# adaLN's middle weight rows in a two-layer diffusion backbone: six moved to the first branch, eighteen behind the second branch's second unit

## The chip, the cores and the metric

One core of a Trainium2 chip runs the whole program. The metric is the time of one execution on the device in microseconds; less is better. Three executions of the kernel before gave 2494.15 us at the median (2492.76 to 2498.52). The profile is of one further execution.

## The reference, cut to what matters

Two post-norm layers work on 640 tokens of width 1024 (128 context tokens, 512 latent ones). Everything is float32, and a product of two matrices is done as three products of rounded parts (high by high, high by low, low by high).

```python
sh1, sc1, g1, sh2, sc2, g2 = split(silu(cond) @ w_ada + b_ada, 6)      # adaLN, 6144 columns
h = x * (1 + sc1) + sh1
r_out, s_out, n_out = retention(h), s5(h), attention(h)               # three mixers of one projection
m = (ga * (r_out @ wb[0]) + gb * (s_out @ wb[1]) + gc * (n_out @ wb[2])) @ w_o
x = layer_norm(alpha * x + g1 * m)
x = layer_norm(alpha * x + g2 * conv_ffn(x * (1 + sc2) + sh2))
```

The condition has one vector for the context tokens (`c_ctx`) and one for the latent ones (`c`). The state-space mixer (`s5`) has a scan over 80 blocks of 8 tokens, then outputs, a gelu, and a gated unit: `y * sigmoid(y @ w_glu)`. Its result goes through the second branch product.

## The kernel before, in words

**The stream of units.** `layer` writes out a list of units. A unit names the weight tiles that it needs (128 by 1024 float32, 512 KB each) and emits its instructions. Projections (`a_unit`, `gate_unit`), the gated unit (`glu_unit`, L1262 to L1288) and branch products (`branch_unit`, L1298 to L1332) take one tile per unit; 48 matmuls of 128x320 make a unit of about 7 us on TensorE. Around the change the order is: eight gates of the first branch, its four branch units, four gates of the second branch (with `ssm_out`, the gelu of the state-space mixer, put ahead of the third), two gated units, then the four units of the second branch with the other four gates among them, then the query and key projections of the attention.

**The weight ring.** `load_to` (L202) issues the loads on the SyncE queue in the order of the list into a ring of four `raw` buffers (`NRAW`). `split_to` (L210) makes a high part on ScalarE (L176) and a low part on VectorE (L177), into three pairs of buffers (`NHL`). A tile of the kind `raw` is not split: it keeps its raw buffer until the instructions that use it are done. The next tile in the list takes whichever buffer comes free first.

**adaLN as rows.** The first 16 blocks of 128 columns of layer 0 are done by matmuls at the start. All others are done by VectorE in `ada_rows` (L297 to L314). A row unit loads one tile of `w_adaT` (two blocks of 128 columns by 512 inputs) and takes four products with sums against the two silu rows `crow` (L308, 128x512 each). Each block needs two such units, one for either half of the inputs; the second also adds to the first and the bias (L311, L312). `cond_rows(i)` (L278 to L289) makes the two rows `crow` for half `i` of the inputs: a load on the POOL queue (L285), a tanh on ScalarE (L286) and two instructions on VectorE (L287, L288) each.

**Where rows go.** `build` mixes the row units into the list by `spread`, which puts `extra` evenly behind the units of a stretch. The middle rows of a layer (blocks 16 to 39) are 26 entries: 12 units of the first half, `cond_rows(1)`, 12 units of the second half, and the release of `crow`. They begin at `s.rows_at` (L1581). Their results are needed at the third branch (`make_gate`) and at the output projection (`scales`), much later.

**The scan.** In both layers the scan of the state-space mixer is a chain of 64 steps of four VectorE instructions (L1194 to L1197). Behind it come `ssm_outputs` (copies at L1224, matmuls at L1238 and L1240, `ym` at L1241, stores at L1245) and `ssm_out` (loads at L1254, gelu at L1256, the split into `gyhi` and `gylo`), and then the gated unit (matmuls at L1273).

**The order on an engine.** The context is made with `schedule_with_timeline_sim=True`: the build gives each engine's queue its order by a timeline of its own, in which an instruction may go ahead of earlier ones of the list that aren't ready. On the chip the queue is then followed as it stands.

Of the kernel before, what the change touches and what calls it, by code (L numbers as in the profile page):

```python
# [80 lines left out]
class Kernel:  # L81
# [1389 lines left out]
    def layer(s, l):  # L1471
        nc, A, O = s.nc, s.A, s.O
        units = []
# [92 lines left out]
        for h in range(4):  # L1566
            add(s.rg_unit(l, h, need=[rets[h]]))
        for c in range(8):
            if c == 6:
                add(s.action(lambda: s.cond_rows(0)))  # L1570
            add(s.gate_unit(l, 0, c))
        for i in range(4):
            add(s.branch_unit(l, 0, i))

# [3 lines left out]
            add(s.gate_unit(l, 1, c))  # L1578
        for i in range(2):
            add(s.glu_unit(l, i))  # L1580
        s.rows_at = len(units) + 1  # L1581
        for i in range(4):
            for c in (2 * i, 2 * i + 1) if i > 1 else ():
                add(s.gate_unit(l, 1, c))
            add(s.branch_unit(l, 1, i))
        c = 0
# [134 lines left out]
    def build(s):  # L1721
        s.adac, s.bcol, s.gate, s.ret, s.ssm, s.ready = {}, {}, {}, {}, {}, set()
        s.rq, s.rk, s.rv, s.rout = {}, {}, {}, {}
        s.nq, s.nk, s.nvd, s.nout = {}, {}, {}, {}
        s.gy, s.sout, s.gts, s.hid, s.chunk = {}, {}, {}, {}, {}
        s.preps = [[None, g, r, 0] for g, r in ((s.first_ssm(), RATE_S), (s.ssm_prep(1), RATE_P))]
        s.ada_begin(0)
        s.setup()
        units = [s.hold(s.win(0, 2)[:2])]

        def first(n):
            s.ada_unit(n)
            s.first_h(n)

        for n in range(4):
            if n < 3:
                units.append(s.action(lambda n=n: s.ada_load(n + 1), start=[] if n else [s.preps[0]]))
            units.append(s.action(lambda n=n: first(n), cost=1))
        def rest():
            s.free(s.cond)  # L1740
            s.cap = len(s.slots)

        units.append(s.action(rest))
        def rows(l, a, b, first):

            r = lambda i, last: [s.ada_rows(l, m, i, last) for m in range(a // 2, b // 2)]
            return r(first, False) + [s.action(lambda: s.cond_rows(1 - first))] + r(1 - first, True)

        s.crow = []
        w = len(TURNS)  # L1750
        done = s.action(lambda: [s.free(s.crow), s.crow.clear()])
        for l in range(s.layers):
            u = [s.action(lambda l=l: s.begin(l))] + s.layer(l)
            find = lambda: [i for i, x in enumerate(u) if x["emit"].__qualname__.endswith("res_unit.<locals>.emit")]
            at = find()
            if l + 1 < s.layers:
                extra = [s.action(lambda l=l: s.ada_begin(l + 1))] + rows(l + 1, 0, 16, 0)
                u = s.spread(u, extra, at[w] + 1, at[-w])
            u = s.spread(u, [s.action(lambda: s.cond_rows(1))] + rows(l, 40, 48, 1), at[w - 1] + ADA[0], at[w - 1] + ADA[2])
            u = s.spread(u, rows(l, 16, 40, 0) + [done], s.rows_at, at[0] - 3 - ADA[1])  # L1760
            u.insert(find()[-w], done)
            units += u
        s.run(units)
# [11 lines left out]
BETWEEN = (0, 0, 0, 8)  # L1775

ADA = (14, 14, 16)

RATE_R, RATE_N, RATE_S, RATE_T, RATE_P = 2.5, 2.75, 1.25, 0.7, 0.5

# [98 lines left out]
```

## Time and profile before

| what | value |
|---|---|
| median of three runs | 2494.15 us (2492.76 to 2498.52) |
| the profiled execution | 2493.69 us |
| its span from first to last instruction | 2491.9 us |
| instructions | 44951 |
| mean granted TensorE clock | 0.983 of full speed |

The span is what the trace shows; the profiled execution's time has 1.8 us around it. In rows of the trace, PE is TensorE's matmuls, PEld its weight loads, DVE VectorE, ACT ScalarE, POOL GpSimd, SP SyncE, and a small q marks an engine's own queue. A number after x counts instructions. What stands in brackets behind `<-` is the work that ended the idle time before. Times count from the span's start.

### The profile page before, as it was taken

To read this page: it belongs to the slowest core of one execution; us is meant where nothing else is said; L and a number is where in the kernel's file an instruction comes from. 1 tells how busy PE (TensorE), PEld (TensorE's weight loads), DVE (VectorE), ACT (ScalarE), POOL (GpSimd) and SP (SyncE) were. 2 spreads that over 40 slices of the span, in tenths; PEclk is the share of its full clock that TensorE was granted. 3 is DMA by queue.
4 is the path that set the end of the run, shared out by engine and by line. 5 is a ranking of instruction groups with operands and counts; after the bars stand their busy time and mean duration, and the time that the engine had idled before them with its cause. 6 is when DMAs were issued, how large, how long until landed. Compare 5 with 4: busy or idle time off the path is not lost.

```text
span 2491.9 us, 44951 instructions
## 1 busy us (share of the span) xinstructions
PE 2391.0 (96%) x17788; PEld 2324.2 (93%) x17788; DVE 1793.1 (72%) x4241; ACT 978.4 (39%) x1713; POOL 414.1 (17%) x676
## 2 busy tenths in 40 slices
PE   6999998999999999999999999999999999999996
PEld 3998998899898999999999999999989999999996
DVE  7986765886667988899684577379667888555647
ACT  2445434245634323222345644422655333232231
POOL 5423222203200002110011120411131000000001
PEclk8999999999999999999999999999999999999998
DMA  8744445643233436444354332555333343212222
GB/s 284 249 152 132 138 130 170 189 143 104 74 97 103 140 100 222 128 159 138 122 171 130 98 111 91 160 171 190 103 92 100 107 138 97 85 57 93 90 64 81
DMA packets 108099, 324.18 MB, mean 130 GB/s; under 512 B 24848, under 2 KB 25680, under 8 KB 107888
## 3 DMA queue, kind: packets, MB, share of 16 engines
q1 hardware_dynamic: 62784, 211.32, 25.9%
q0 software_dynamic: 44672, 109.86, 14.6%
q8 instruction: 140, 2.29, 0.4%
q14 instruction: 71, 0.58, 0.1%
q10 hardware_dynamic: 432, 0.13, 0.0%
HBM read 287.09 MB, written 38.21 MB: 131 GB/s over the span
## 4 chain that ended last, share of the span: by engine, by line
PE 65%; issue 20%; DVE 9%; DMA 4%; ACT 2%; POOL 1%; POOLq 0%; DVEq 0%; ACTq 0%
PE pa L148 35%; PE pa L1311 6%; PE b L1351 2%; PE b L1352 2%; PE b L1353 2%; DMA raw<-in_w_adaT 2%; DVE lo L177 2%; PE pn L859 2%; PE pa L515 1%; PE pa L517 1%; PE pa L516 1%; PE b L757 1%; DVE junk L308 1%; PE b L846 1%; PE b L1173 1%
## 5 line engine op out<-in xcount | busy, mean ns | idle before, releaser
L148 PE MATMUL pa<-hth,hi 128*128 128x320 f32 (+2 forms) x2896 | 683.1, 314 | 21.9 <-DVE cv L1395 8.5
L148 PE MATMUL pa<-htl,hi 128*128 128x320 f32 (+2 forms) x2896 | 681.8, 313 | 3.0 <-DVE htl L396 2.1
L148 PE MATMUL pa<-hth,lo 128*128 128x320 f32 (+2 forms) x2896 | 680.6, 313 | 0.0
L176 ACT ACTIVATE hi<-raw 128x1024 fp32r<-128x1024 f32 (+1 forms) x316 | 322.2, 1022 | 850.9 <-PE pa L148 351.4
L177 DVE TENSOR_TENSOR lo<-raw,hi 128x1024 fp32r<-128x1024 f32 (+1 forms) x316 | 372.4, 1180 | 262.1 <-ACT hi L176 250.9
L148 PEld LDWEIGHTS pa<-hth,hi 128*128 128x128 f32 x2896 | 490.9, 190 | 32.5 <-issue 10.4
L148 PEld LDWEIGHTS pa<-htl,hi 128*128 128x128 f32 x2896 | 493.0, 190 | 9.9 <-DVE htl L396 3.7
L148 PEld LDWEIGHTS pa<-hth,lo 128*128 128x128 f32 x2896 | 493.6, 190 | 1.7 <-issue 1.2
L308 DVE SCALAR_TENSOR_TENSOR junk<-raw,crow 128x512 bf16<-128x512 f32 x320 | 223.3, 698 | 47.6 <-DMA raw<-in_w_adaT 44.0
L1352 PE MATMUL b<-lo,hdh 128*128 128x256 f32 x784 | 218.2, 281 | 0.0
L1353 PE MATMUL b<-hi,hdl 128*128 128x256 f32 x784 | 217.7, 281 | 0.0
L1351 PE MATMUL b<-hi,hdh 128*128 128x256 f32 x784 | 215.0, 282 | 2.2 <-ACT hi L176 2.2
L1395 DVE SCALAR_TENSOR_TENSOR cv<-pa,conv,cv 128x641 f32<-128x641 f32 (+3 forms) x180 | 153.6, 854 | 4.5 <-ACT cv L1391 2.5
L1351 PEld LDWEIGHTS b<-hi,hdh 128*128 128x128 f32 x784 | 145.8, 188 | 3.7 <-ACT hi L176 3.2
L1352 PEld LDWEIGHTS b<-lo,hdh 128*128 128x128 f32 x784 | 147.7, 189 | 0.0
L1353 PEld LDWEIGHTS b<-hi,hdl 128*128 128x128 f32 x784 | 147.4, 189 | 0.0
L1355 DVE TENSOR_TENSOR rm<-b,g 128x256 f32<-128x256 f32 x168 | 69.3, 421 | 74.4 <-PE b L1353 74.0
L515 PE MATMUL pa<-hi,hth 128*128 128x256 f32 x320 | 91.5, 287 | 2.3 <-ACT qk L1482 2.3
L516 PE MATMUL pa<-lo,hth 128*128 128x256 f32 x320 | 90.0, 282 | 0.0
L517 PE MATMUL pa<-hi,htl 128*128 128x256 f32 x320 | 89.3, 282 | 0.0
L1391 ACT ACTIVATE cv<-pa,conv 128x641 f32<-128x641 f32 (+2 forms) x90 | 76.3, 848 | 17.7 <-PE pa L148 14.5
L176 ACT ACTIVATE hdh<-cv 128x641 fp32r<-128x641 f32 x44 | 32.6, 741 | 125.4 <-DVE cv L1403 125.4
(440 smaller groups left out, 4360.9 us busy)
## 6 DMA issues: line engine op xcount, KB each, us to landing
raw<-in_w_in_a SPq DMA_DIRECT2D x96, 512.0 KB, 3.7
raw<-in_w_up SPq DMA_DIRECT2D x88, 512.0 KB, 3.6
raw<-in_w_adaT SPq DMA_DIRECT2D x80, 512.0 KB, 4.2
raw<-in_w_down SPq DMA_DIRECT2D x36, 512.0 KB, 3.5
raw<-in_w_branch SPq DMA_DIRECT2D x24, 512.0 KB, 3.8
raw<-in_w_o SPq DMA_DIRECT2D x24, 512.0 KB, 3.5
wada<-in_w_ada SPq DMA_DIRECT2D x32, 256.0 KB, 6.1
raw<-in_w_in_b SPq DMA_DIRECT2D x16, 512.0 KB, 4.6
```

The source lines that it names most:

```text
L148: s.nc.tensor.matmul(ps[h][:, :n], w[a][:, k], x[b][:, k, c0:c0 + n], start=(k == 0 and part == 0), stop=(k == nk - 1 and part == 2))
L176: s.nc.scalar.activation(hi, src, AF.Copy)
L177: return (eng or s.nc.vector).tensor_tensor(lo, src, hi.bitcast(FT), op=OP.subtract)
L308: nc.vector.scalar_tensor_tensor(junk, w[:, n], 1.0, s.crow[j], op0=OP.mult, op1=OP.mult, accum_out=acc[:, n, j:j + 1])
L515: mm(ps, h[0], x[0], start=(k == 0), stop=False)
L516: mm(ps, h[0], x[1], start=False, stop=False)
L517: mm(ps, h[1], x[0], start=False, stop=(k == 7))
L1311: nc.tensor.matmul(ps[:, h, :n], w[a][:, k, 128 * c:128 * c + 128], out[k][x][:, c0:c0 + n], start=(k == 0 and part == 0), stop=(k == 3 an ...
L1351: mm(ps, a[0], x[0], start=(k == 0), stop=False)
L1352: mm(ps, a[0], x[1], start=False, stop=False)
L1353: mm(ps, a[1], x[0], start=False, stop=(k == nk - 1))
L1395: nc.vector.scalar_tensor_tensor(x[:, o0:o1], z[:, z0:z0 + o1 - o0], cw(tap), x[:, o0:o1], op0=OP.mult, op1=OP.add)
```

## The change

Three things are edited. `cond_rows(0)`, the silu of the first half of the conditions, is put ahead of the fifth gate of the first branch rather than the seventh. `s.rows_at` becomes a list of two places: the last gate of the first branch, and the first gate behind the second branch's second unit. Of the 26 middle entries the first six row units go to the first place, one behind each of six units (the last gate, the four units of the first branch, the first gate of the second branch); the other twenty (eighteen row units, `cond_rows(1)` and the release) are spread over the twelve units from the second place on, to the same end as before. The rows themselves, their count and their order are unchanged.

```diff
         for c in range(8):
-            if c == 6:
+            if c == 4:
                 add(s.action(lambda: s.cond_rows(0)))
             add(s.gate_unit(l, 0, c))
+        s.rows_at = [len(units)]
         for i in range(4):
             add(s.branch_unit(l, 0, i))
...
         for i in range(2):
             add(s.glu_unit(l, i))
-        s.rows_at = len(units) + 1
         for i in range(4):
+            if i == 2:
+                s.rows_at.append(len(units) + 1)
             for c in (2 * i, 2 * i + 1) if i > 1 else ():
                 add(s.gate_unit(l, 1, c))
             add(s.branch_unit(l, 1, i))
...
-            u = s.spread(u, rows(l, 16, 40, 0) + [done], s.rows_at, at[0] - 3 - ADA[1])
+            middle = rows(l, 16, 40, 0) + [done]
+            u = s.spread(u, middle[EARLY:], s.rows_at[1], at[0] - 3 - ADA[1])
+            u = s.spread(u, middle[:EARLY], s.rows_at[0], s.rows_at[0] + EARLY)
...
 ADA = (14, 14, 16)
+
+EARLY = 6
```

## Rows read from the trace of the kernel before

**Rows 1.** The page, busy time of each engine

```profile
PE 2391.0 (96%) x17788; PEld 2324.2 (93%) x17788; DVE 1793.1 (72%) x4241; ACT 978.4 (39%) x1713; POOL 414.1 (17%) x676
```

**Rows 2.** Stretches: length, busy us of PE, PEld, DVE, ACT, POOL; PEclk, DMA, GB/s

```profile
350.00:400.00 50.00, 50.00 (x376) 50.00 (x375) 18.81 (x41) 30.57 (x34) 23.92 (x41) 1.00 0.53 169
...
415.00:470.00 55.00, 42.58 (x234) 40.27 (x233) 40.64 (x83) 16.38 (x20) 10.79 (x17) 0.84 0.55 160
...
1650.00:1680.00 30.00, 27.56 (x180) 26.23 (x180) 27.13 (x55) 7.74 (x11) 8.97 (x13) 1.00 0.77 208
```

**Rows 3.** Waits of TensorE, 360 to 560 us: in total, times, longest

```profile
PE pa L1311 <- DVE solo L1283: 4.2, 2, 3.4
PE pa L1273 <- DVE gylo L177: 4.0, 2, 2.9
PE pa L1273 <- ACT gyhi L176: 2.5, 2, 1.5
PE pa L1311 <- ACT sohi L1282: 1.1, 1, 1.1
PE pa L1311 <- DVE gt L1315: 0.6, 1, 0.6
```

**Rows 4.** Timeline of TensorE, 439 to 448 us: start, length, what

```profile
439.12 0.46 PE L1311 MATMUL pa<-sohi,hi 128*128 128x320 f32 x2
...
444.19 0.74 PE L1311 MATMUL pa<-sohi,lo 128*128 128x320 f32 x2
444.72 0.73 PE L1311 MATMUL pa<-sohi,hi 128*128 128x320 f32 x2
...
447.48 0.45 PE L1311 MATMUL pa<-sohi,hi 128*128 128x320 f32 x2
447.77 0.46 PE L1311 MATMUL pa<-solo,hi 128*128 128x320 f32 x2
```

**Rows 5.** VectorE's timeline: two adaLN rows' first products

```profile
392.99 0.69 DVE L308 SCALAR_TENSOR_TENSOR junk<-raw,crow 128x512 bf16<-128x512 f32 x1 [1.07 <-DMA raw<-in_w_adaT]
...
450.44 0.69 DVE L308 SCALAR_TENSOR_TENSOR junk<-raw,crow 128x512 bf16<-128x512 f32 x1 [4.80 <-DMA raw<-in_w_adaT]
```

**Rows 6.** The page, group of line 308

```profile
L308 DVE SCALAR_TENSOR_TENSOR junk<-raw,crow 128x512 bf16<-128x512 f32 x320 | 223.3, 698 | 47.6 <-DMA raw<-in_w_adaT 44.0
```

**Rows 7.** Timelines of VectorE and SyncE, 295 to 297 us

```profile
295.42 1.23 DVE L177 TENSOR_TENSOR lo<-raw,hi 128x1024 fp32r<-128x1024 f32 x1 [0.34 <-ACT hi L176]
...
296.67 0.33 SPq L206 DMA_DIRECT2D raw<-in_w_branch  x1
```

**Rows 8.** VectorE's timeline in the second layer's scan

```profile
1497.35 0.22 DVE L1197 TENSOR_TENSOR H<-H,rc 128x64 f32<-128x64 f32 x1
1497.61 0.23 DVE L1194 TENSOR_TENSOR rc<-H,ssm_ar 128x64 f32<-128x64 f32 x1
...
1498.47 0.22 DVE L1197 TENSOR_TENSOR H<-H,rc 128x64 f32<-128x64 f32 x1
1498.61 0.69 DVE L288 TENSOR_TENSOR crow<-crow,crt 128x512 f32<-128x512 f32 x1
1499.21 0.22 DVE L1194 TENSOR_TENSOR rc<-H,ssm_ar 128x64 f32<-128x64 f32 x1
```

**Rows 9.** Timelines: scan's end and last gylo in each layer; first gated matmul

```profile
354.87 0.23 DVE L1197 TENSOR_TENSOR H<-H,rc 128x64 f32<-128x64 f32 x1
...
427.85 0.82 DVE L177 TENSOR_TENSOR gylo<-gy,gyhi 128x640 fp32r<-128x640 f32 x1
...
1545.63 0.23 DVE L1197 TENSOR_TENSOR H<-H,rc 128x64 f32<-128x64 f32 x1
...
1616.10 0.82 DVE L177 TENSOR_TENSOR gylo<-gy,gyhi 128x640 fp32r<-128x640 f32 x1
...
1639.97 0.46 PE L1273 MATMUL pa<-gyhi,hi 128*128 128x320 f32 x2
```

**Rows 10.** The page, DMA issues: size each, us to landing

```profile
raw<-in_w_adaT SPq DMA_DIRECT2D x80, 512.0 KB, 4.2
```

## The prediction

> **What bounds the kernel now.** I read the page's busy times first. TensorE is busy 96% of the span [rows 1], so an edit that moves VectorE work can only win back TensorE's idle time, or add to it. Then I cut the span into stretches to see where that idle time lies. Around the change, TensorE is full from 350 to 400 us and again after 470, but from 415 to 470 it is busy 42.58 of 55 us at a granted clock of 0.84; the same place in the second layer, 1650 to 1680, loses 2.44 us at full clock [rows 2]. So the first layer's gated unit and the second branch's first units hold 12.4 us of idle time, and some slow clock. The table of waits names who is late: `gylo` and `gyhi`, the gelu's split (6.5 us), then `solo`, `sohi` and `gt`, the gated unit's output and the branch's evacuation (5.9 us) [rows 3].
>
> Third, the timeline shows what a wait costs beyond itself. Behind one, pairs of matmuls start 0.53 us apart (444.19, 444.72) where they later start 0.29 apart (447.48, 447.77) [rows 4]: the lower of the two clocks, 1.2 GHz, then the higher, 2.4. I count 6 slow pairs after 443.5 and 11 after 454.6, 17 x 0.24 = 4.1 us.
>
> Fourth, VectorE's timeline. adaLN rows stand in the list behind the second branch's first unit, whose matmuls begin at 439.12 [rows 4]; the first row runs at 392.99 [rows 5], 46 us earlier. **A unit's place in the list is thus not its place in a queue**: the build lets rows go ahead as soon as the ring has a buffer. And it seems to count on a quicker load than the chip's. VectorE sat idle 1.07 us before that row and 4.80 before the one at 450.44, with the gated unit's last `solo` queued behind it [rows 5]; over all 80 rows such waits make 44.0 us [rows 6].
>
> **The change, part by part.** *Silu sooner.* Two loads on the POOL queue, two tanh and four VectorE instructions go ahead by two gates. Ends: 0, and 4 x 0.48 = 1.9 us if they newly enter the scan (price below). I take 0: in the second layer such an instruction already stands within the scan [rows 8]. The price of a late `crow` would be rows stuck in the ring with weights queued behind them on SP.
>
> *Six rows at the first branch.* Where do they land? A freed raw buffer goes to the next tile in the list: a split ends at 295.42 + 1.23 = 296.65, and SP issues the next load, a branch weight, at 296.67 [rows 7]. In the new list the first early row stands just ahead of that weight, so it takes this load, and with 4.2 us to landing [rows 10] it can run from about 301. A row holds its buffer only some 8 us (4.2 plus its work), so the next ones follow closely: I put all six between 301 and 355. That is **the scan, which ends at 355.1** [rows 9], and not the idle stretch behind it (18.8 us busy of 50 from 350 to 400 [rows 2]). Does other work cut into the scan? The second layer shows it: between two dependent steps 0.26 us apart (1497.35, 1497.61) a `crow` product of 0.69 us is put in, and the steps stand 0.74 apart (1498.47, 1499.21) [rows 8]. An insertion thus costs 0.48. Six rows are 24 products of the same 0.69-0.70 us: 24 x 0.48 = **+11.5 us**. Ends: 0 (all wait for the idle stretch) and 6 x 2.8 = 16.8 (whole length, 223.3 / 80 = 2.8 us a row [rows 6]). I take the `crow` price: same length, same chain.
>
> *Their waits for landing.* Ends: 0, and 6 x 1.07 = 6.4, the idle time before the first row now [rows 5]; the 4.80 stands for a single row. I take the mean of all rows, 44.0 / 80 = 0.55, because there is scan work to put into a load's time: 6 x 0.55 = **+3.3**.
>
> SP's order is otherwise safe: by the code a weight is loaded up to four raw buffers and three split pairs ahead of its matmuls, units of about 7 us each, so one row between two weights starves nothing.
>
> *Who waits for the scan.* Its outputs, their stores and loads, the gelu, `gylo`, the gated unit. From the scan's end to the last `gylo`'s end: 428.67 - 355.10 = 73.6 us in the first layer, 1616.92 - 1545.86 = 71.1 in the second [rows 9], so this chain keeps its length whatever runs beside it, and TensorE waits for its end in the first layer [rows 3]: a late scan is a late gated unit, one for one. In the second layer the gated matmuls begin at 1639.97 [rows 9], 23 us behind the last `gylo`, and a scan late by 15 costs nothing there.
>
> *Rows taken from the gated unit.* Fewer rows in front of `gylo`: I take the second layer's length of the chain, where none stand: 71.1 - 73.6 = **-2.5** (ends 0 and -6.5, all of that wait [rows 3]). At the second branch's first units: ends 0 and -(5.9 + 4.1) = -10.0. I take half the idle part, **-3**, since the ring still lets later rows go ahead as soon as the second branch's weights are split, and the silu of the second half comes there as before. Second layer: **-2** of 2.44 [rows 2] (ends 0 and -2.44). The stretch to 560 has 18 rows in twelve units where it had 20 behind the same gate; TensorE has no idle time there, so 0.
>
> Sum: 2493.69 + 11.5 + 3.3 - 2.5 - 3 - 2 = **2501.0 us**. The profiled execution is 0.5 below the median and within the runs' spread; I leave it at 2501.
>
> **Two rules weighed.** An insertion costs 0.48 us by rows 8. The Trainium skill (VectorE: DVE Perf Modes, "The DRAIN you can't avoid") says that the next VectorE op does not start until the pipeline of the one before is empty, though it adds that an instruction that isn't held starts earlier; by the strict rule each product would cost its 0.69, 24 x 0.69 = 16.5, and the sum would be 2506; in rows 8 the inserted product starts 0.14 after a 0.22 us instruction, so the trace sides with the exception. A load of 512 KB lands in 4.2 us by rows 10. The Trainium skill (SBUF — State Buffer, "The DMA setup-cost knee") fits about 2 us plus bytes at 436 GB/s, an estimate of 3.2 us here; with that the early rows would hardly wait and the sum would lose its 3.3.
>
> **The rivals.** (a) *Rows keep out of the scan* and use the idle stretch behind it. For it: 31 us idle against 17 of rows. Against: 296.67 and rows 8, and nothing in the list ties rows to the scan's end. Sum: 2493.69 - 2.5 - 3 - 2 = 2486.2, faster; it decides if the scan is late by less than 2.5 us. (b) *A draw*: the scan is late as forecast, but the second branch gives back all 10.0 instead of 3, as its rows run while TensorE waits for the chain: 2494.0. (c) *Full price*: an inserted row costs its whole 2.8 us: 2501.0 + 5.3 = 2506.3. The drain rule named above would work this way. (d) *The gated unit doesn't empty*: eighteen rows listed later go ahead to it all the same, as the old ones did by 46 us: neither 2.5 nor 3 comes back, 2506.5. This is the change not doing what it says.
>
> **How the numbers follow.** About 0.2% (5 us: 2489.2 to 2499.1) is what a measurement of this kernel can tell from no change. Chances: forecast 0.35, (a) 0.24, (b) 0.20, (c) 0.10, (d) 0.11. Of the forecast 0.27 lies above the band and 0.08 within it, by its open ends at the second branch; of (a) 0.22 below and 0.02 within; of (b) 0.18 within and 0.02 below; (c) and (d) above. Faster 0.24, same 0.28, slower 0.48. The forecast's own range is 2495 to 2507. The whole range, 2484 to 2511, reaches from (a) with 2 us more at the second branch, past (c) and (d), to the forecast with landing waits and price both near their upper ends (+3.1 and +5.3); left out are (a) with all the idle time won and a scan late by both upper ends with nothing given back.
>
> **What would show it.** In the changed kernel's trace: L308 products between L1194 and L1197 from about 301; the scan's end near 370, not 355; the last `gylo` near 441; TensorE idle ahead of it by more than the 6.5 us of rows 3; `solo` waits shorter; the second layer without idle time at the gated unit. I am wrong if the scan still ends by 358, if first-branch rows run only behind it, or if TensorE waits for a weight's split between 300 and 370. A gated unit that is late with the scan on time would mean another link of the chain, such as POOL's stores behind a silu load.

## The result and the profile after

| what | before | after |
|---|---|---|
| median | 2494.09 us (4 runs, 2492.76 to 2498.52) | 2510.09 us (4 runs, 2507.59 to 2511.53) |
| span of the profiled execution | 2491.9 us | 2507.3 us |

The change makes the kernel 16 us slower: ratio 1.0065, 95% interval 1.0052 to 1.0079. The forecast was +7.

The windows of the changed kernel, with the columns of [rows 2]:

```profile
350.00:400.00 50.00, 46.54 (x329) 45.84 (x327) 26.80 (x94) 23.02 (x26) 13.43 (x24) 0.98 0.42 129
415.00:470.00 55.00, 42.63 (x278) 40.03 (x276) 33.16 (x65) 19.59 (x24) 15.50 (x25) 0.97 0.50 146
1650.00:1680.00 30.00, 29.22 (x198) 28.69 (x196) 21.36 (x44) 12.25 (x16) 6.58 (x10) 1.00 0.50 140
```

TensorE still loses 12.4 us between 415 and 470, and it now loses 3.5 between 350 and 400, where it was full. The windows stand still, though, and the stage has moved: the gated unit's first matmul starts at 429.17 where it started at 415.34. So here are the stretch from the last `gylo`'s end to the attention's first transpose at L846 (first layer), and 40 us from the first gated matmul on (second layer), before and after:

```profile
428.67:545.40 116.73, 110.80 (x710) 109.18 (x711) 100.97 (x245) 35.93 (x70) 20.11 (x26) 0.94 0.57 175
1639.97:1680.00 40.03, 37.59 (x249) 36.26 (x248) 35.67 (x76) 12.40 (x17) 8.97 (x13) 1.00 0.70 195
```

```profile
444.79:561.30 116.51, 107.87 (x704) 104.98 (x705) 91.67 (x222) 35.55 (x70) 18.03 (x26) 0.97 0.52 162
1657.66:1697.70 40.04, 37.93 (x256) 37.14 (x255) 34.32 (x70) 14.05 (x18) 9.56 (x14) 1.00 0.65 184
```

The second branch takes as long as before (116.7 and 116.5 us): TensorE idles 2.7 us more there and, at a granted clock of 0.97 instead of 0.94, is busy 2.9 less. Its waits from 360 to 560 in the changed kernel (compare [rows 3]):

```profile
PE pa L1273 <- DVE gylo L177: 4.7, 2, 3.5
PE pa L1273 <- ACT gyhi L176: 3.6, 1, 3.6
PE pa L1311 <- DVE gt L1315: 3.2, 2, 2.7
PE b L1238 <- DMA gm<-md: 3.0, 2, 1.6
PE pa L1311 <- DVE solo L1283: 2.3, 1, 2.3
```

The gated unit's inputs are late by 8.3 us instead of 6.5, and `gm`, a load of the state-space outputs, is a new name. Now the scan. The timeline of VectorE in the changed kernel, at the first products of five of the six early rows (the other row had no such wait), then the last step of the scan and the last `gylo` of the first layer, then of the second:

```profile
300.19 0.69 DVE L308 SCALAR_TENSOR_TENSOR junk<-raw,crow 128x512 bf16<-128x512 f32 x1 [1.36 <-DMA raw<-in_w_adaT]
...
312.74 0.69 DVE L308 SCALAR_TENSOR_TENSOR junk<-raw,crow 128x512 bf16<-128x512 f32 x1 [4.90 <-DMA raw<-in_w_adaT]
...
323.00 0.69 DVE L308 SCALAR_TENSOR_TENSOR junk<-raw,crow 128x512 bf16<-128x512 f32 x1 [2.22 <-DMA raw<-in_w_adaT]
...
331.08 0.69 DVE L308 SCALAR_TENSOR_TENSOR junk<-raw,crow 128x512 bf16<-128x512 f32 x1 [0.35 <-DMA raw<-in_w_adaT]
...
344.33 0.69 DVE L308 SCALAR_TENSOR_TENSOR junk<-raw,crow 128x512 bf16<-128x512 f32 x1 [0.22 <-DMA raw<-in_w_adaT]
...
375.74 0.23 DVE L1197 TENSOR_TENSOR H<-H,rc 128x64 f32<-128x64 f32 x1
...
443.97 0.82 DVE L177 TENSOR_TENSOR gylo<-gy,gyhi 128x640 fp32r<-128x640 f32 x1
...
1577.34 0.22 DVE L1197 TENSOR_TENSOR H<-H,rc 128x64 f32<-128x64 f32 x1
...
1647.19 0.83 DVE L177 TENSOR_TENSOR gylo<-gy,gyhi 128x640 fp32r<-128x640 f32 x1 [1.36 <-ACT gyhi L176]
```

All six rows run inside the scan. It ends at 375.97 instead of 355.10 [rows 9], 20.9 us late. The last `gylo` ends at 444.79 instead of 428.67, 16.1 us late, and the kernel is 16.0 us slower. The page's group of line 308 shows the loads' side (compare [rows 6]): waits for landing tiles grew from 44.0 to 71.1 us.

```profile
L308 DVE SCALAR_TENSOR_TENSOR junk<-raw,crow 128x512 bf16<-128x512 f32 x320 | 222.8, 696 | 74.0 <-DMA raw<-in_w_adaT 71.1
```

**What fills the longer scan.** I cut one window in each kernel, from 268 us to the scan's end, and compared VectorE's busy time and its groups of instructions. First the windows, before and after:

```profile
268.00:355.10 87.10, 87.10 (x651) 86.33 (x650) 74.55 (x290) 27.72 (x39) 13.28 (x24) 1.00 0.38 125
```

```profile
268.00:375.97 107.97, 104.86 (x760) 103.82 (x759) 91.94 (x343) 28.69 (x39) 13.26 (x24) 0.98 0.44 142
```

VectorE's groups in these windows (count, then busy us and mean ns, then the idle time before them), before and after:

```profile
L177 DVE TENSOR_TENSOR lo<-raw,hi 128x1024 fp32r<-128x1024 f32 x12 | 14.7, 1223 | 5.7 <-ACT hi L176 5.7
L1315 DVE SCALAR_TENSOR_TENSOR gt<-gt,pa 128x640 f32<-128x640 f32 x4 | 3.3, 822 | 1.7 <-PE pa L1311 1.7
```

```profile
L177 DVE TENSOR_TENSOR lo<-raw,hi 128x1024 fp32r<-128x1024 f32 x14 | 17.1, 1219 | 0.8 <-ACT hi L176 0.6 <-issue 0.2
L308 DVE SCALAR_TENSOR_TENSOR junk<-raw,crow 128x512 bf16<-128x512 f32 x24 | 16.5, 686 | 9.1 <-DMA raw<-in_w_adaT 9.1
L1315 DVE SCALAR_TENSOR_TENSOR gt<-gt,pa 128x640 f32<-128x640 f32 x8 | 6.6, 819 | 2.3 <-PE pa L1311 2.3
```

The 20.9 us are 17.4 more busy (91.94 - 74.55) and 3.5 more idle (16.03 - 12.55, each the window less its busy time). Of the busy part, two more weight splits (2.4) and four more branch evacuations (3.3) are not adaLN's at all. TensorE went on with the first branch while the scan lasted longer, and its evacuations and splits now stand ahead of the scan's last steps: 5.7 us. That leaves 17.4 - 5.7 = 11.7 for the 24 products, 0.49 each. Of the idle part, 9.1 us of waits for tiles are new, but the waits for `hi` fell from 5.7 to 0.6: most of the new idle time stands where old idle time was.

### The profile page after: what moved, and what is told of

Same layout as the page of the kernel before. It is cut to its first block, busy times and chain, and to the rows that moved or that the text cites. A ratio compares the mean times of both kernels' runs of the same rounds, so it can differ in the third digit from the quotient of the medians.

```text
span 2507.3 us, 44929 instructions
## 1 busy us (share of the span) xinstructions
PE 2395.0 (96%) x17788; PEld 2324.1 (93%) x17788; DVE 1789.8 (71%) x4241; ACT 978.5 (39%) x1713; POOL 409.0 (16%) x676
## 3 DMA queue, kind: packets, MB, share of 16 engines
q0 software_dynamic: 44672, 109.86, 14.8%
## 5 line engine op out<-in xcount | busy, mean ns | idle before, releaser
L148 PEld LDWEIGHTS pa<-hth,hi 128*128 128x128 f32 x2896 | 490.6, 190 | 37.3 <-issue 11.8
L308 DVE SCALAR_TENSOR_TENSOR junk<-raw,crow 128x512 bf16<-128x512 f32 x320 | 222.8, 696 | 74.0 <-DMA raw<-in_w_adaT 71.1
L1351 PE MATMUL b<-hi,hdh 128*128 128x256 f32 x784 | 215.1, 282 | 2.3 <-ACT hi L176 2.2
L1351 PEld LDWEIGHTS b<-hi,hdh 128*128 128x128 f32 x784 | 145.9, 188 | 4.1 <-ACT hi L176 3.2
L1391 ACT ACTIVATE cv<-pa,conv 128x641 f32<-128x641 f32 (+2 forms) x90 | 76.4, 848 | 17.8 <-PE pa L148 11.5
```

Of the source, the lines that this page charges most:

```text
L148: s.nc.tensor.matmul(ps[h][:, :n], w[a][:, k], x[b][:, k, c0:c0 + n], start=(k == 0 and part == 0), stop=(k == nk - 1 and part == 2))
L308: nc.vector.scalar_tensor_tensor(junk, w[:, n], 1.0, s.crow[j], op0=OP.mult, op1=OP.mult, accum_out=acc[:, n, j:j + 1])
L1351: mm(ps, a[0], x[0], start=(k == 0), stop=False)
L1391: nc.scalar.activation(x[:, a:b], z[:, a - base:b - base], AF.Identity, scale=cw(1), bias=cw(3))
```

## Experiments

The runs come in four groups, and each group has its own median of the kernel before: 2493.97 (the first four), 2493.30 (the next four), 2493.27 (three) and 2492.80 us (the last). Ratios are to that median.

**No early rows.** All 24 rows at the later place, silu sooner as in the change.

```diff
-            u = s.spread(u, middle[EARLY:], s.rows_at[1], at[0] - 3 - ADA[1])
-            u = s.spread(u, middle[:EARLY], s.rows_at[0], s.rows_at[0] + EARLY)
+            u = s.spread(u, middle, s.rows_at[1], at[0] - 3 - ADA[1])
```

> No early rows at all: all 24 middle row units go behind the second branch's second unit (the first place is dropped), the silu stays at the fifth gate. Theory S (the six early rows inside the first layer's scan make the whole loss): the first layer's scan ends near 355 us again, and the time is 2484 to 2496, no slower than the kernel before. Rival P (the second place makes the loss: rows crowded behind the second branch's second unit, VectorE full, weights late): the time stays at 2502 to 2515, or is above the changed kernel's.

Measured: 2490.67 us, ratio 0.9998 (0.9985 to 1.0011); the scan ends at 354.82. The loss is gone, so it hangs on the early rows, and neither the later place nor the earlier silu costs anything that this run can tell.

**Second layer only.** The first layer as before.

```diff
-            if c == 4:
+            if c == (4 if l else 6):
...
-                s.rows_at.append(len(units) + 1)
+                s.rows_at.append(len(units) + 1 if l else len(units) - 1)
...
-            u = s.spread(u, middle[EARLY:], s.rows_at[1], at[0] - 3 - ADA[1])
-            u = s.spread(u, middle[:EARLY], s.rows_at[0], s.rows_at[0] + EARLY)
+            early = EARLY if l else 0
+            u = s.spread(u, middle[early:], s.rows_at[1], at[0] - 3 - ADA[1])
+            u = s.spread(u, middle[:early], s.rows_at[0], s.rows_at[0] + early)
```

> The change made in the second layer alone; the first layer has its old list. Theory S: rows stand in the second layer's scan too, but 23 us of slack hide it, so the time is within 0.2% of the kernel before (2489 to 2497). Rival L (both layers pay, each about half): 2499 to 2505.

Measured: 2495.03 us, ratio 1.0003 (0.9995 to 1.0012). In the changed kernel the second layer's scan is late as well, but its gated matmuls begin 9.6 us behind the last `gylo` (1657.66 against 1648.02). The loss belongs to the first layer: the interval leaves at most 3 us to the second.

**Six rows behind the scan.** They stand behind the third and fourth gate of the second branch.

```diff
-        s.rows_at = [len(units)]
...
+                s.rows_at = [len(units) + 2]
                 add(s.action(s.ssm_out, need=[ssm]))
...
-            u = s.spread(u, middle[:EARLY], s.rows_at[0], s.rows_at[0] + EARLY)
+            u = s.spread(u, middle[:EARLY], s.rows_at[0], s.rows_at[0] + 2)
```

> The six early rows moved from the first branch to behind the third and fourth gate of the second branch (three each), so that the ring can give them a buffer only as the first layer's scan ends; the other eighteen stay as in the changed kernel. Theory S: the scan ends by 359 us, the first rows run in VectorE's idle stretch behind it, and the time is 2485 to 2495. If instead any six rows ahead of the gated unit cost what they cost in the changed kernel, wherever they run (rival E), the time is 2502 to 2512.

Measured: 2491.45 us, ratio 0.9984 (0.9970 to 0.9999). The time is in S's range, but the scan ends at 361.81 and not by 359: 7 of the 24 products went ahead into it all the same. With its scan 6.7 us late this kernel is no slower than before.

**The gated unit emptied.** As that run, with the other eighteen rows behind the second branch's last unit and ending eight units later.

```diff
-            if i == 2:
-                s.rows_at.append(len(units) + 1)
...
+        s.rows_at.append(len(units))
         c = 0
...
-            u = s.spread(u, middle[EARLY:], s.rows_at[1], at[0] - 3 - ADA[1])
+            u = s.spread(u, middle[EARLY:], s.rows_at[1], at[0] + 5 - ADA[1])
```

> As the run with six rows behind the third and fourth gate, and the other eighteen go behind the second branch's last unit, ending eight units later, so that no row can reach the gated unit or the second branch. Theory W (row loads that VectorE waits for are what holds the gated unit and the second branch's units): the 12.4 us of idle time from 415 to 470 us shrink below 6, and the time is 2476 to 2486, below the kernel before. Rival C (the chain of stores, loads and gelu holds the gated unit, rows or not): the idle time stays above 9, and the time is 2487 to 2495.

Measured: 2494.07 us, ratio 0.9998 (0.9987 to 1.0009), above what W expects. The trace shows where the gain went: the windows of this run, columns as in [rows 2],

```profile
415.00:470.00 55.00, 49.96 (x326) 48.26 (x326) 33.42 (x47) 18.30 (x22) 17.68 (x25) 0.97 0.48 124
560.00:750.00 190.00, 181.64 (x1372) 169.02 (x1372) 140.05 (x362) 90.06 (x220) 37.11 (x50) 0.98 0.41 124
```

The idle time at the gated unit did shrink, from 12.4 to 5.0 us. But the attention's transposes at L846 now last from 531.6 to 680.3 (148.7 us; before 139.0), and in the second layer 157.3 us (before 145.0). The output projection of the first layer starts 5.2 us early (706.8 for 712.0), and the second layer's attention uses that up.

**Early rows without loads.**

```diff
-            w = tiles[0][0].rearrange("p (n k) -> p n k", n=2)
+            w = tiles[0][0].rearrange("p (n k) -> p n k", n=2) if tiles else None
...
-                    nc.vector.scalar_tensor_tensor(junk, w[:, n], 1.0, s.crow[j], ...
+                    nc.vector.scalar_tensor_tensor(junk, w[:, n] if tiles else s.crow[n], 1.0, s.crow[j], ...
...
+            for x in middle[:EARLY]:
+                x["slots"] = []
```

> The changed kernel, but its six early rows load nothing: their products read the silu rows instead of weight tiles, so their results are not adaLN's. Theory I+W: the scan is late by two parts, 24 insertions of about 0.49 us (11.8 us) and 9.0 us of waits for landing tiles, and the time follows the scan with some 5 us of slack. Then the scan ends near 367 (before 355.1, changed kernel 376.0), no product in it waits for a load, and the time is about 2501 (2497 to 2504). Rival W alone (only the waits cost, the products fill VectorE's idle time): the scan ends by 358 and the time is 2491 to 2496. Rival I alone (the waits were covered anyway): the scan ends at 374 or later and the time is 2507 to 2512.

Measured: 2510.49 us, ratio 1.0069 (1.0051 to 1.0087). The scan's last step in this run, and VectorE's groups in it, from 268 us to its end:

```profile
373.21 0.22 DVE L1197 TENSOR_TENSOR H<-H,rc 128x64 f32<-128x64 f32 x1
```

```profile
L177 DVE TENSOR_TENSOR lo<-raw,hi 128x1024 fp32r<-128x1024 f32 x14 | 17.1, 1220 | 4.2 <-ACT hi L176 4.2
L1315 DVE SCALAR_TENSOR_TENSOR gt<-gt,pa 128x640 f32<-128x640 f32 x8 | 6.6, 822 | 3.4 <-PE pa L1311 3.4
```

Without a single wait for a tile, the scan is late by 18.3 us, and the loss is the whole loss. I+W falls, and with it my reading of the waits as a cost of their own; the time is in I's range, and the scan ends 0.6 us short of I's 374. The same two extra splits and four extra evacuations are there. VectorE's busy time in the scan grew by 18.6, so the products take 18.6 - 5.7 = 12.9, 0.54 each, and its idle time is 12.3 where it was 12.55.

**Loads without products.**

```diff
+            if emit.__dict__.get("small"):
+                nc.vector.tensor_copy(out, w[:, :, :2])
-            for n in range(2):
+            for n in range(0 if emit.__dict__.get("small") else 2):
...
+            for x in middle[:EARLY]:
+                x["emit"].__dict__["small"] = True
```

> The changed kernel, but each early row, which still loads its tile, takes one copy of 128x4 from it in place of its four products, so adaLN's columns of six row units are left out. Theory I+W: only the waits are left. They are at least the 9.0 us of the changed kernel, since no products of a row lie within the next load; the scan ends at 363 to 368 and the time is 2497 to 2504. Rival I alone: the scan ends by 358 and the time is 2491 to 2496. Rival W alone: the scan ends at 374 or later, and the time is 2507 to 2512.

Measured: 2488.09 us, ratio 0.9974 (0.9962 to 0.9987). The waits of VectorE from 285 to 400 us in this run, and the scan's last step (two lines lower in this file):

```profile
DVE adac L307 <- DMA raw<-in_w_adaT: 11.9, 6, 3.8
```

```profile
358.68 0.23 DVE L1199 TENSOR_TENSOR H<-H,rc 128x64 f32<-128x64 f32 x1
```

VectorE stood 11.9 us for tiles, more than the 9.1 of the changed kernel, and the scan is late by only 3.8. So **a wait that holds the scan is not a delay of the scan in full**: while VectorE stands, the next `hi` and the next product of TensorE become ready, and the waits for them fall away (up to the scan's end VectorE waited 0.6 us for `hi` and nothing for `gt`, where before it waited 5.7 and 1.7). In the scan the two runs bound the loads' part: 2.6 us is what is missing without them (20.9 - 18.3), 3.8 what they do alone. In the time, the products and what follows them carry the loss.

**Three early rows.** `EARLY = 3`.

> Three early rows in place of six, the other 21 at the later place. Theory I+W counts the first three rows of the changed kernel's trace: waits of 1.36, 4.90 and 2.22 us and 12 insertions of 0.49 us make 14.4, so the scan ends near 369.5, and with some 5 us of slack the time is about 2503 (2500 to 2506). Rival N (every row costs the same, half the rows cost half): the scan ends near 365.5 and the time is about 2502. The scan's end tells them apart, not the time. Rival E (the loss does not depend on the number of rows but on VectorE's queue being held at all): 2507 to 2512.

Measured: 2504.13 us, ratio 1.0056 (1.0035 to 1.0078); the scan ends at 365.05, as N has it and not I+W, though its three waits were 9.0 us, more than I+W counted. The last `gylo` ends at 438.26.

**Rows before the attention.** The gated unit emptied as above, with the old end.

```diff
-            u = s.spread(u, middle[EARLY:], s.rows_at[1], at[0] + 5 - ADA[1])
+            u = s.spread(u, middle[EARLY:], s.rows_at[1], at[0] - 3 - ADA[1])
```

> The kernel with six rows behind the scan and eighteen behind the second branch's last unit, but the eighteen end where they end in the kernel before, not eight units later. In the run with the later end TensorE's first L846 product of the first layer came at 531.6 (before: 545.4), but its last one at 680.3 (before: 684.4), so 9.7 of 13.8 us were lost between them. Theory B: the rows among the attention's first units lost them, by holding its VectorE steps. Then here the first L846 is at 531 to 537, the last at 671 to 677, and the time is 2484 to 2489. Rival D (the attention has work of its own that bounds it there, or the denser rows ahead of it now hold the branch): the last L846 is at 679 or later and the time is 2490 to 2496.

Measured: 2500.73 us, ratio 1.0030 (1.0017 to 1.0043). B falls, and D's number is passed as well: L846 runs from 530.4 to 683.5. The largest group of TensorE's waits from 470 to 750 us is new:

```profile
PE pa L148 <- ACT hi L176: 5.1, 2, 3.8
```

TensorE waits for weight splits of the projections. Eighteen row loads packed between those weights is what the edit adds there; that they delay the weights was not tried by itself. Nor do these waits make the loss: at the first L1351, the output projection of the first layer, this run is still 1.1 us ahead of the kernel before (710.9 for 712.0). It falls behind in the second layer's attention, whose transposes at L846 last 160.9 us (1742.4 to 1903.3) where they lasted 145.0; why is open.

**First layer behind the scan.** Six rows one gate later still, eighteen behind the second branch's last unit with the later end; the second layer as before.

```diff
-            if c == 4:
+            if c == (6 if l else 4):
...
-        s.rows_at = [len(units)]
...
+                s.rows_at = [len(units) + 3]
                 add(s.action(s.ssm_out, need=[ssm]))
...
-            if i == 2:
+            if l and i == 0:
                 s.rows_at.append(len(units) + 1)
...
+        if not l:
+            s.rows_at.append(len(units))
...
-            u = s.spread(u, middle[EARLY:], s.rows_at[1], at[0] - 3 - ADA[1])
-            u = s.spread(u, middle[:EARLY], s.rows_at[0], s.rows_at[0] + EARLY)
+            early = 0 if l else EARLY
+            u = s.spread(u, middle[early:], s.rows_at[1], at[0] + (-3 if l else 5) - ADA[1])
+            u = s.spread(u, middle[:early], s.rows_at[0], s.rows_at[0] + 2)
```

> First layer alone: six rows behind the fourth gate of the second branch (all of them behind the scan's last step in VectorE's queue), the other eighteen behind the second branch's last unit with the later end; silu sooner; the second layer as in the kernel before. In the run that had the like in both layers, the output projection's first L1351 product came 5.2 us earlier in the first layer (706.8 for 712.0), and the gain was lost in the second layer's attention. Theory G (the gated unit's idle time is worth some 5 to 8 us, in the first layer alone): the scan ends at 355 (three rows inside it made 361.8), the first L1351 comes at 703 to 707, the time is 2485 to 2490. Rival D (VectorE's queue between the scan and gylo has no room for the six rows either): the last gylo is late by 5 us or more, and the time is 2491 to 2496.

Measured: 2486.26 us, ratio 0.9976 (0.9965 to 0.9986): **faster than both kernels**, 7 us below before and 24 below the change. The scan's last step, the last `gylo` and the last `solo` on VectorE's timeline, then the window:

```profile
356.48 0.22 DVE L1197 TENSOR_TENSOR H<-H,rc 128x64 f32<-128x64 f32 x1
...
426.76 0.83 DVE L177 TENSOR_TENSOR gylo<-gy,gyhi 128x640 fp32r<-128x640 f32 x1 [3.76 <-ACT gyhi L176]
...
442.08 0.82 DVE L1283 SCALAR_TENSOR_TENSOR solo<-glt,sohi 128x640 fp32r<-128x640 f32 x1 [0.80 <-ACT sohi L1282]
```

```profile
415.00:470.00 55.00, 51.53 (x329) 50.41 (x327) 33.50 (x47) 19.66 (x24) 17.42 (x24) 0.94 0.44 122
```

The six rows run in the idle stretch behind the scan, no row stands between `gylo` and `solo`, and TensorE idles 3.5 us there where it idled 12.4. Not all of the gain stands there: of the profiled execution's 9.4 us (a span of 2482.5 for 2491.9) 4.3 are there at the first L1351 (707.7 for 712.0), and no run tells what made the rest.

**The eighteen at the change's place.** The same six rows; the others as in the change, first layer only.

```diff
-            if l and i == 0:
+            if i == (0 if l else 2):
                 s.rows_at.append(len(units) + 1)
...
-            u = s.spread(u, middle[early:], s.rows_at[1], at[0] + (-3 if l else 5) - ADA[1])
+            u = s.spread(u, middle[early:], s.rows_at[1], at[0] - 3 - ADA[1])
```

> As the run before, but the eighteen rows of the first layer begin behind the second branch's second unit, as in the changed kernel, and end as there. It is the change with its six rows moved from the scan to the idle stretch behind it. Theory G of the prediction's rival (a): the six cost nothing there and the eighteen leave part of the gated unit's idle time free, so the time is 2486 to 2490. Rival H (eighteen rows listed later go ahead to the gated unit all the same): TensorE's idle time from 415 to 470 stays at 11 us or more, and the time is 2492 to 2497.

Measured: 2492.43 us, ratio 1.0000 (0.9986 to 1.0014). H holds: the window from 415 to 470 has 43.92 us of TensorE, 11.1 idle. Rows at 413.86, 420.28, 428.33, 434.94 and 444.25 stand among `gylo` and `solo`, with waits up to 2.54 us, though the list puts them behind the second branch's second unit. This pair of runs differs in the place of eighteen rows alone, and in 6.2 us; their first L1351 are 6.2 us apart as well.

**Early rows left out.**

```diff
+            if emit.__dict__.get("none"):
+                nc.gpsimd.memset(out, 0.0)
+                return
...
+            for x in middle[:EARLY]:
+                x["emit"].__dict__["none"], x["slots"] = True, []
```

> The changed kernel with its six early row units left out of both layers: neither load nor product, their six pairs of adaLN's columns are set to zero. What is left of the change is eighteen rows at the later place and the silu sooner. Theory S (all the loss comes through the late scan, and taking six rows from the gated unit and the second branch gives back about the 5 us seen with loads only): the scan ends at 354 to 356, the time is 2484 to 2489, and the early rows cost 21 to 26 us. Rival L (part of the loss comes from the later place itself): the time is 2492 or more.

Measured: 2495.37 us, ratio 1.0007 (0.9995 to 1.0019), as L expects, so what is left of the change brings nothing. But S's condition wasn't met: the scan ends at 362.21 without any row in it. One more retention evacuation (three instructions) and one more split stood in it, and the waits for `hi` were 9.3 us. The build had drawn another order, and the scan is 7.1 us late by that.

**Three early rows without loads.** The run without loads with `EARLY = 3`.

> Half the dose of the run without loads: three early rows whose products read the silu rows (their results are not adaLN's), the other 21 rows at the later place. Against the run with three early rows it lacks their loads alone. The scan: 12 products at 0.5 us make 6, and other units' instructions that then fall into it some 2 more, so it ends near 363 (before 355.1, six without loads 373.4, three with loads 365.0). Theory K (the path behind the scan has slack: scans later by 4 to 7 us cost nothing in four runs, later ones cost what goes beyond): the time is 2493 to 2498. Rival O (one for one from the first microsecond, the four runs having won as much elsewhere): the time is 2500 to 2504.

Measured: 2507.62 us, ratio 1.0055 (1.0036 to 1.0073); the scan ends at 363.86, as forecast, and both theories miss the time. The last `gylo` shows where the time went:

```profile
442.80 0.82 DVE L177 TENSOR_TENSOR gylo<-gy,gyhi 128x640 fp32r<-128x640 f32 x1 [3.38 <-ACT gyhi L176]
```

It ends 79.8 us behind the scan, where before needs 73.6 and the run with the first layer behind the scan 70.9. Part of it is a wait: ScalarE's last copies of the scan's state (L1224, at 388.38) wait 8.2 us for TensorE's products at L1240, where the like wait was 3.1 us before and 4.7 in the changed kernel. Why the build's order makes it longer stays open. Against the run without loads, half the products make 86% of the loss (14.8 of 17.2): the loss isn't so much per product.

**All runs in one table** (us, all of the first layer; first L1351 is the start of its output projection; the last column is the median against that of before in the same group):

| kernel | scan ends | last `gylo` ends | between | first L1351 | time |
|---|---|---|---|---|---|
| before | 355.1 | 428.7 | 73.6 | 712.0 | |
| changed | 376.0 | 444.8 | 68.8 | 729.8 | +16.0 |
| early, no loads | 373.4 | 445.6 | 72.1 | 726.8 | +17.2 |
| three, no loads | 363.9 | 443.6 | 79.8 | 728.4 | +14.8 |
| three early | 365.1 | 438.3 | 73.2 | 720.0 | +10.8 |
| left out | 362.2 | 435.9 | 73.7 | 715.5 | +2.1 |
| eighteen at the old gate | 356.9 | 432.0 | 75.0 | 713.9 | -0.8 |
| six behind the scan | 361.8 | 431.6 | 69.8 | 711.1 | -2.5 |
| loads only | 358.9 | 431.2 | 72.3 | 714.9 | -5.2 |
| gated unit empty | 361.8 | 428.9 | 67.1 | 706.8 | +0.1 |
| rows before the attention | 362.5 | 429.7 | 67.2 | 710.9 | +7.4 |
| second layer only | 354.4 | 428.1 | 73.7 | 709.9 | +1.1 |
| no early rows | 354.8 | 426.4 | 71.5 | 709.1 | -3.3 |
| first layer behind scan | 356.7 | 427.6 | 70.9 | 707.7 | -7.0 |

The big losses go with the last `gylo` of the first layer, not with the scan's end. The four kernels that end it later than 437 are the four that lose 10 us or more, and their loss is its delay within 1.3 us. The others don't keep that order: their `gylo` is between 2.3 us early and 7.2 late, and the time is up to 8 us off that delay (loads only: 2.5 late and 5.2 faster; left out: 7.2 late and 2.1 slower). The two kernels with the emptied gated unit in both layers lie on the slow side, and both have a longer attention in the second layer (157.3 and 160.9 us for 145.0).

## Why the prediction came out as it did

The direction and the mechanism were right, the size was not: +7 forecast, +16 measured. The median of 2510.09 lies above the forecast's own range (to 2507) and above every rival's sum (2506.5 at most); even the forecast with landing waits and price at their upper ends makes 2509.4 (2501.0 + 3.1 + 5.3). That the whole range, to 2511, holds it is luck: the reason given for its upper end is not what happened. Step by step:

- *Where the six rows land*: right. From 300.19 (forecast 301), all inside the scan. Rival (a) fell.
- *Silu sooner*: taken as 0, right. The run without early rows has it, and its scan ends at 354.82.
- *Insertion*: right. 0.48 was taken, 0.49 came out of the windows (0.54 in the run without loads): 11.7 us for 11.5. The Trainium skill's rule (VectorE: DVE Perf Modes, "The DRAIN you can't avoid"), read strictly, would make 0.69 each and 16.5; the windows don't bear that out.
- *Landing waits*: taken as 3.3; the scan has 3.5 us more idle time, but not for the reason given, so the match is luck. The waits were 9.1 us, above the term's upper end of 6.4, and the waits for `hi` shrank by 5.1 beside them. The run without loads lost as much as the change. The Trainium skill's setup-cost fit (SBUF — State Buffer, "The DMA setup-cost knee"; an estimate of 3.2 us for this tile) stands against a median of 4.0 us in this stretch, and by the run without loads the time didn't hang on which of the two holds.
- **The missing term**: other units' work that a longer scan lets in, +5.7. The sum counted what is inserted and left the rest of VectorE's queue in place. But TensorE's first branch runs on, and its splits and evacuations come ahead of the scan's late steps. VectorE was busy 74.55 of 87.10 us there, so there was little room for it. In the runs the count goes with the scan's end: 12 splits and 4 evacuations where it ends at 355, 12 and 5 at 358.9, 12 and 6 at 361.8, 13 and 7 at 363.9 and 365.1, 14 and 8 at 373.4 and 376.0. The split of the 20.9 us is still a reading of one pair of orders: with the rows left out, the build's order alone moved the scan's end by 7.1 us.
- *The chain behind the scan keeps its length*: failed. It was 68.8 in the changed kernel and between 67.1 and 79.8 in the others. The -2.5 became -4.8. Rows ahead of `gylo` don't explain it: the chains of 68.8 and of 79.8 us both have them.
- *The second branch gives back 3*: failed, 0 (116.7 us before, 116.5 after). TensorE's waits for `solo` fell as forecast, from 4.2 to 2.3 us, but those for `gt` at L1311 rose from 0.6 to 3.2. This is rival (d)'s mechanism. Rows listed behind the second unit ran at 424.55 (5.34 us of wait), 431.20, 441.15, 447.71 and 457.57 in the changed kernel, among `gylo` and `solo`. Moving the place by a unit or two takes no row out of the gated unit: 17 row products run between its start and the last `solo` before and in the run without early rows, 16 in the changed kernel. Putting the place behind the last unit does (3.5 us idle against 11.1).
- *Second layer -2*: failed. The window of [rows 2] has 0.8 us of idle time instead of 2.4, but the gated unit starts 17.7 us later there; from its first matmul on, 2.1 us are left. The run with the change in the second layer only is +1.1 us, an interval that holds no change.

With the measured terms: 11.7 + 5.7 + 3.5 - 4.8 = +16.1. They are parts of the last `gylo`'s delay, so they add up to it by the way they were taken; that the median moved by as much, +16.0, is the finding. The forecast's terms in the scan gave 14.8 where 20.9 came, and its gains of 5 us behind the gated unit didn't come. The prediction's "one for one" fits the four slow kernels, from the last `gylo` on and not from the scan's end; the other kernels, with delays of up to 7 us, don't follow it.

One loss wasn't foreseen at all: at 347.58 TensorE waits 3.11 us for an evacuation `gt` of the first branch that stands behind row products on VectorE. The prediction looked only at weight splits there.

## What to carry to other kernels

A long chain of small steps on an engine with an ordered queue paid twice here for what was put into it: for the insertion, and for the steady work of the other stages that arrived while the chain lasted longer. Count the engine's whole queue up to the chain's end, busy and idle, not the insertion alone. Waits are to be counted net, against the idle time that the stretch already has. And a place in a list moves nothing unless the order that the build makes of it moves: read where the instructions stand in the queue (here a step from one unit to another changed nothing, a step past the whole stage won 6 us), then put filler work into the idle stretch behind the chain.

## What the runs showed of the chip that was not expected

A row's tile can take much longer than the page's median. The second early load is issued at 304.84 on SyncE's queue and its product starts at 312.74, 7.9 us later; the median to landing in 295 to 350 us is 4.0. In that time the core was moving other tiles: the view of the transfers from 295 to 350 us, cut into 40 slices of 1.375 us, stands at 402 GB/s in the three slices from 307.4 to 311.5. That they were the cause was not tried. The rates, then the group of these loads (KB each, median us to landing), both of the changed kernel:

```profile
GB/s 54 313 419 84 3 45 262 215 289 402 402 402 361 101 6 98 274 280 366 137 0 0 89 292 167 215 69 313 0 152 247 60 340 197 241 206 188 292 27 119
```

```profile
raw<-in_w_adaT SPq DMA_DIRECT2D x6, 512.0 KB, 4.0
```

And the same lateness shows in two shapes. From 290 us to the first L1351, TensorE's window in the changed kernel, in the run without loads and in the kernel before:

```profile
290.00:729.80 439.80, 410.42 (x2889) 390.82 (x2888) 289.04 (x801) 187.68 (x395) 99.23 (x155) 0.97 0.42 128
```

```profile
290.00:726.80 436.80, 416.13 (x2896) 398.52 (x2895) 290.23 (x804) 187.83 (x395) 100.37 (x155) 0.95 0.40 122
```

```profile
290.00:712.00 422.00, 404.29 (x2894) 387.71 (x2894) 295.98 (x804) 188.11 (x395) 101.61 (x155) 0.98 0.43 134
```

The changed kernel has 11.7 us more idle and 6.1 more busy time at a mean granted clock of 0.97; the run without loads has 3.0 more idle and 11.8 more busy at 0.95. With nearly the same count of matmuls, the second one stood less and ran slower. Whoever counts TensorE's idle time alone sees 3.0 of 14.8 us in the one and 11.7 of 17.8 in the other.
